# A two-layer decoder trunk on one core: late transposes, first stick-breaking scores, compressor outputs and second-branch scores stand further behind what feeds them

## The chip, the cores and the metric

The kernel runs on one core of one Trainium2 chip. The metric is the device time of one execution in microseconds. Three runs of the kernel before took 648.68, 647.72 and 650.42 us, a median of 648.68 us. One more execution was taken with the hardware profiler on; the rows below come from that one.

## The reference, cut to what matters

`x` is 256 x 1024 float32, one sequence. There are two layers, each a token mixer and an MLP, each behind an RMSNorm and added back to `x`, and a last RMSNorm.

```python
def reference(x, ...):
    for layer in range(2):
        h = rmsnorm(x, attn_norm[layer])
        x = x + (sb_diff_mixer if layer == 0 else nsa_mixer)(h, ...)
        x = x + squared_relu_mlp(rmsnorm(x, mlp_norm[layer]), mlp_w1[layer], mlp_w2[layer])
    return rmsnorm(x, final_norm)
```

Layer 0 has 8 stick-breaking heads (logits z = q k, weights exp(log sigmoid(z) + the sum of log sigmoid(-z) over later keys)) beside 4 differential heads. Layer 1 is native sparse attention: 16 heads in 4 groups with three branches, each with its own keys and values, merged by sigmoid gates: compressed blocks (blocks of 32 keys, stride 16, plus a position term, go through `gelu(flat @ w1) @ w2`), selected blocks (256 positions are 4 blocks and 16 may be taken, so all are), and a window of 512 (all positions again). Both MLPs are `square(relu(h @ w1)) @ w2` with 4096 hidden columns.

## The kernel before, in words

Everything is float32 but carried as a high and a low part: a product with a weight is three matmuls, high weight by high and by low activation and low weight by high activation. `Weights` loads each weight in halves on SP's queue, ACT casts the high part (`wh`, line 76) and DVE subtracts the low part (`wl`, line 80), some buffers ahead of use. All of TensorE's products go through `mm` (line 122), so most of its rows carry L122 and the tiles tell them apart. A scheduler works from the order in which the program issues its steps and what each waits for; it moves single instructions by a few places, so the place in the program is not all that sets the order on an engine.

Activations are kept transposed, 128 features by 256 tokens, in two token halves t=0 and t=1. After each residual add, `norm_full` or `norm_deferred` makes the scaled `xg` of one token half on DVE; `transposed` (line 408) puts four 128x128 transposes in one PSUM tile `ps_t` (line 413), ACT casts the high part and DVE subtracts the low part (lines 400 and 401). For t=0 that is done at once; for t=1 it is put on the list `late`, and `run_late` issues it among the next stage's products, so that these cover the norm of t=1.

The places that the change touches, in order of time:

- **Layer 0's mixer** (`even_mixer`): `halves(i, a, b, q, k)` projects half i of the queries and then half i of the keys of one branch, each as two tiles `ps_f` (m=0, 1) of 24 products, which ACT copies to `qsb` and `ksb` (line 647). `sb_start` issues the logits `z` of two head pairs, 16 products of 64 rows and 8 of a mask, and ACT and DVE make a softplus of them, split in high and low (`sb_e`, `sb_sp`, `sb_h`, `sb_l`, lines 717 to 722). `sb_weights` later multiplies these with a triangle of ones into the same `z`. The order is `halves(0)`, `sb_start` for pairs 0 and 1, `halves(1)`, `sb_weights`.
- **Both MLPs** (`mlp`): the first two chunks (c=0, 1) of the up projection run one token half at a time (`up_tile`, 24 products into `ps_ut`: 16 with the high weight, 8 with the low one), so that t=0 can start before t=1 is there. `run_late` issues the transposes of t=1 between (c=0, t=0) and (c=1, t=0), two groups of four. The other 14 chunks take both halves at once.
- **The entry of layer 1** (`odd_mixer`): the down projection of the first MLP (`macc`, `project_rows`) ends t by t and half by half; behind it `norm_full` and the transposes of t=0, then the value projections `ps_vs` and `ps_vw` of t=0, `run_late`, and those of t=1.
- **Layer 1's order block**: keys, queries and the two compressors (keys, then values) are projected, and softmax work of the four groups is mixed in. `run(a, b)` takes steps from two generators in turn. `scores(g, b)` issues the logits `s` of group g in branch b for both token halves, and `soft` their softmax (DVE line 1124, ACT line 1127, POOL line 1132); `cmp_scores` the compressed branch (`sc`, `pc`). `compress_blocks` projects `ps_c` (two tiles of 24 products) and transposes the positions (`ps_pos`, line 1012); `compress_hidden` gives `ps_h`; `compress_gelu` copies it out (`hc`, line 1045), adds its halves with 4 matmuls into `ps_hT` (through `fold`) and takes a gelu; `compress_keys` and `compress_values` multiply with w2 into `ps_co`. `values(i)` transposes the softmax of pair i (`pt`, line 1176; `ptc`) and issues the products with the values of pair i-1 (`o`).

```python
hk = self.compress_gelu(0, h[0], up)
run(self.compress_blocks(1, xT, up, pool, f))
run(queries(1), once(lambda: soft(scores(0, 1))))
run(self.compress_hidden(f[1], h[1]))
soft(scores(1, 0))
self.compress_keys(hk, f[0], kd)
hv = self.compress_gelu(1, h[1], up)
q2 = queries(2)
next(q2)
run(part(q2, KT))
soft(cmp_scores(0))
soft(scores(1, 1))
self.compress_values(hv, f[1], vc)
run(part(q2, KT), values(0))
```

Of the kernel before, what the change touches and what calls it, by code (L numbers as in the profile page):

```python
# [10 lines left out]
F32 = mybir.dt.float32  # L11
# [7 lines left out]
P = 128  # L19
# [80 lines left out]
class Trunk:  # L100
# [323 lines left out]
    def norm_full(self, t, n, dst):  # L424

        v = self.square_half(t, n)
        if n == 0:
            self.xg = self.tmp.tile([P, D], F32, tag="xg", name="xg")
        xg = self.xg
        self.half_gain(xg, t, n)  # L430
        if n == 0:
            return
        rs = self.rsqrt(v)
        for i in range(2):
            c = slice(i * 512, i * 512 + 512)
            self.nc.vector.tensor_scalar(xg[:, c], xg[:, c], rs, None, op0=ALU.mult)
        self.later(t, lambda: [self.transposed(t, i, xg, dst) for i in range(2)])

# [6 lines left out]

    def run_late(self):
        for f in self.late:
            f()
        self.late = []

# [30 lines left out]

    def tmajor(self, ps, w, x, t, kts, first, last, cs=slice(None)):

        wh, wl = w
        tq = slice(t * P, (t + 1) * P)
        terms = ((x[0], wh), (x[1], wh), (x[0], wl))
        for j, (a, b) in enumerate(terms):
            for i, kt in enumerate(kts):
                self.mm(ps, a[:, kt, tq], b[:, i, cs], first and i == j == 0, last and j == 2 and i == len(kts) - 1)

    def project_rows(self, o, w, act, r, t, n, first, last):

        c = slice(n * 512, n * 512 + 512)
        tq = slice(t * P, (t + 1) * P)
        for i in range(2):
            kt = 2 * r + i
            h, l = act(kt)
            self.mm(o, h[:, tq], w[0][:, i, c], kt == first, False)
            self.mm(o, h[:, tq], w[1][:, i, c], False, False)
# [9 lines left out]
    def finish_rows(self, acc, ws, act, first, last, scale, after):  # L509

        for t in range(2):
            for n in range(2):
                o = acc[t][n]
                for r, w in ws:
                    self.project_rows(o, w, act, r, t, n, first, last)
                self.add_residual(t, n, o, scale)
# [36 lines left out]
    def mlp(self, l, xT, after):  # L553
        nc = self.nc
        with self.tc.tile_pool(name=f"mlp{l}", bufs=4) as pool, \
# [23 lines left out]

            def up_tile(c, w, t):  # L580

                ps = self.bankB("ps_ut")
                self.tmajor(ps[:, :S], w, xT, t, range(8), True, True)
                r = pool.tile([P, S], F32, tag="r", name="r")
# [18 lines left out]
            for t in range(2):  # L603
                for c, w in ((0, w0), (1, w1)):
                    if len(rest) == 1 and t == 0:
                        self.run_late()
                    rest.append(up_tile(c, w, t))
                    if len(rest) > 1:
# [14 lines left out]
    def even_mixer(self, xT, oT, pool, out):  # L623
# [17 lines left out]

        def project_f(key, i, dst, scale):
            w = self.W.get((key, i))
            for m in range(2):
                ps = self.bankB("ps_f")
                self.fmajor(ps[:, :S], w, m, xT)
                nc.scalar.activation(dst[:, 2 * i + m, :], ps[:, :S], AF.Copy, scale=scale)

        def halves(i, a, b, q, k):
            project_f(a, i, q, 0.125)  # L650
            project_f(b, i, k, 1.0)
# [6 lines left out]
        with self.tc.tile_pool(name="ps_sb", bufs=2, space=PSUM) as banks:  # L658
            sb = self.sb_start((0, 1), qsb, ksb, pool, banks)
            halves(1, "sbq", "sbk", qsb, ksb)  # L660
            w = {pr: self.sb_weights(sb[pr], pool) for pr in (0, 1)}
# [150 lines left out]
    def odd_mixer(self, xT, oT, pool, out):  # L812
# [18 lines left out]
        for t in range(2):  # L831
            if t:
                self.run_late()
            ps = self.bankB("ps_vs")
            self.tmajor(ps[:, :S], ws, xT, t, range(8), True, True)
            nc.scalar.copy(v2[:, t, 0, :], ps[:, :S])
            ps = self.bankB("ps_vw")
            self.tmajor(ps[:, :304], w0, xT, t, range(4), True, False)
            self.tmajor(ps[:, :304], w1, xT, t, range(4, 8), False, True)
            nc.vector.tensor_copy(v2[:, t, 1, :], ps[:, :S])  # L840
# [20 lines left out]
        with self.tc.tile_pool(name="nsa", bufs=1) as up, \  # L861
# [56 lines left out]
            run(self.compress_hidden(f[0], h[0]))  # L918
            hk = self.compress_gelu(0, h[0], up)
            run(self.compress_blocks(1, xT, up, pool, f))  # L920
            run(queries(1), once(lambda: soft(scores(0, 1))))
            run(self.compress_hidden(f[1], h[1]))
            soft(scores(1, 0))
            self.compress_keys(hk, f[0], kd)
            hv = self.compress_gelu(1, h[1], up)
            q2 = queries(2)
            next(q2)
            run(part(q2, KT))
            soft(cmp_scores(0))
            soft(scores(1, 1))  # L930
            self.compress_values(hv, f[1], vc)
            run(part(q2, KT), values(0))
            q3 = queries(3)
            next(q3)


            run(values(1, lambda: cmp_scores(1)), part(q3, 4))
            run(values(2, lambda: scores(2, 0)), part(q3, 6))
            run(values(3, lambda: scores(2, 1)), part(q3, 6))
            rows = self.out_rows("odo", oT)  # L940
# [99 lines left out]

    def compress_gelu(self, kv, hp, up):

        nc = self.nc
        hc = up.tile([P, S], F32, tag="hc", name="hc", bufs=1)
        nc.scalar.copy(hc, hp[:, :S])
        pt = self.bankB("ps_hT")
# [162 lines left out]
    def run(self):  # L1209
        nc, a, tc = self.nc, self.a, self.tc  # L1210
        self.rs2 = {}
        self.x = self.const.tile([P, 2, D], F32, name="x")
        self.late = []
        self.weight_order()
# [91 lines left out]
```

## Time and profile before

| | |
|---|---|
| median of three runs | 648.68 us (647.72 to 650.42) |
| the profiled execution's own time | 653.47 us |
| its span | 651.8 us (1.67 us lie around it) |
| TensorE (PE) busy | 636.0 us, 98% of the span |
| VectorE (DVE) busy | 423.1 us, 65% |
| ScalarE (ACT) busy | 344.4 us, 53% |
| GpSimd (POOL) busy | 42.9 us, 7% |
| weights and data read from HBM | 106.39 MB |

A row of the timeline gives the start in us from the span's start, the busy time, the engine, the line, the operation with its output and inputs, the shapes, how many instructions of that kind stand in a row, and in brackets how long the engine had been idle before and what ended that. A busy time runs to the modelled end of the last instruction, and the next matmul starts before that end; so the length of a piece of work is best taken from its start to the start of what comes behind it. A granted clock of 1.00 is TensorE's full clock.

### The profile page before, as it was taken

What the parts mean: (1) busy time and instruction counts of PE and PEld (TensorE: products, weight loads), DVE (VectorE), ACT (ScalarE), POOL (GpSimd) and SP (SyncE); (2) the same over time, 40 slices, a digit from 0 to 9 for tenths busy, and PEclk for the clock granted to TensorE, in tenths of its full rate; (3) what the DMA queues carried; (4) which work ended last, traced back from release to release, by engine and by line L of the source; (5) the groups of instructions that cost most, each with busy time, mean ns of one, the idle gap of its engine ahead of it and who ended that gap; (6) DMA issues with size and microseconds to landing.
All of it is one profiled execution on the core that took longest, in us unless ns stands there. A gap on an engine that the chain in (4) does not pass through costs nothing.

```text
span 651.8 us, 10223 instructions
## 1 busy us (share of the span) xinstructions
PE 636.0 (98%) x3805; PEld 539.7 (83%) x3805; DVE 423.1 (65%) x863; ACT 344.4 (53%) x689; POOL 42.9 (7%) x137
## 2 busy tenths in 40 slices
PE   8999999999999999999999999999999999999995
PEld 4888997898888888888998888777888888888883
DVE  5763768786666666666876566766766666666634
ACT  4674656565444444453656554744564454445423
POOL 4000000000000000000203231440000000000000
PEclk9999999999999999999999979999999999999998
DMA  7774453375665556554798322205366565555501
GB/s 256 228 227 130 132 189 109 121 230 190 191 197 181 196 176 193 190 182 122 226 327 256 115 65 65 66 1 162 124 213 194 182 194 181 188 182 191 192 1 65
DMA packets 74132, 108.11 MB, mean 166 GB/s; under 512 B 5057, under 2 KB 60385, under 8 KB 74082
## 3 DMA queue, kind: packets, MB, share of 16 engines
q1 hardware_dynamic: 74080, 107.45, 51.4%
q8 instruction: 30, 0.49, 0.3%
q14 instruction: 20, 0.16, 0.1%
q10 hardware_dynamic: 2, 0.00, 0.0%
HBM read 106.39 MB, written 1.05 MB: 165 GB/s over the span
## 4 chain that ended last, share of the span: by engine, by line
PE 90%; DVE 3%; DMA 3%; ACT 3%; issue 1%; SPq 0%; ACTq 0%; DVEq 0%
PE macc L122 27%; PE ps_up L122 24%; PE ps_f L122 5%; PE acc L122 5%; PE ps_q L122 4%; PE ps_ut L122 3%; PE ps_v L122 3%; DMA w<-in_ev_w_in_dram 3%; PE o L122 2%; PE s L122 2%; PE ps_or L122 2%; PE ps_c L122 2%; PE pt L1176 2%; PE ps_k L122 2%; PE z L122 1%; DVE wl L80 1%
## 5 line engine op out<-in xcount | busy, mean ns | idle before, releaser
L80 DVE TENSOR_TENSOR wl<-w,wh 128x1024 fp32r<-128x1024 f32 (+1 forms) x190 | 227.0, 1212 | 122.2 <-ACT wh L76 121.9
L76 ACT CAST wh<-w 128x1024 fp32r<-128x1024 f32 (+1 forms) x188 | 191.4, 1043 | 91.9 <-PE macc L122 31.5
L122 PE MATMUL ps_up<-m,wh 128*128 128x512 f32 x448 | 159.2, 398 | 0.0
L122 PE MATMUL ps_up<-m,wl 128*128 128x256 f32 x448 | 125.7, 281 | 0.0
L122 PEld LDWEIGHTS ps_up<-m,wh 128*128 128x128 f32 x448 | 84.2, 188 | 20.3
L122 PE MATMUL macc<-wh,l 128*128 128x512 f32 x256 | 100.9, 394 | 0.0
L122 PE MATMUL macc<-wl,h 128*128 128x512 f32 x256 | 100.2, 391 | 0.0
L122 PE MATMUL macc<-wh,h 128*128 128x512 f32 x256 | 99.9, 390 | 0.0
L122 PEld LDWEIGHTS ps_up<-m,wl 128*128 128x128 f32 x448 | 84.6, 189 | 1.1
L577 ACT CAST h<-s 128x256 fp32r<-128x256 f32 x56 | 22.8, 407 | 78.8 <-DVE s L576 78.7
L122 PEld LDWEIGHTS macc<-wh,h 128*128 128x128 f32 x256 | 48.1, 188 | 10.8
L122 PEld LDWEIGHTS macc<-wl,h 128*128 128x128 f32 x256 | 48.1, 188 | 10.0
L122 PEld LDWEIGHTS macc<-wh,l 128*128 128x128 f32 x256 | 48.1, 188 | 10.0
L122 PE MATMUL ps_f<-x,wh 128*128 128x256 f32 x256 | 46.4, 284 | 0.0
L578 DVE TENSOR_TENSOR l<-s,h 128x256 fp32r<-128x256 f32 x56 | 23.8, 425 | 25.5 <-ACT h L577 25.5
L122 PEld LDWEIGHTS ps_f<-x,wh 128*128 128x128 f32 x256 | 39.9, 192 | 0.4 <-issue 0.3
L122 PE MATMUL ps_f<-x,wl 128*128 128x256 f32 x128 | 36.2, 283 | 0.0
L1132 POOL TENSOR_SCALAR p<-p,sums 128x128 f32<-128x128 f32 (+1 forms) x64 | 30.2, 491 | 88.0 <-DVE sums L1130 60.2
L1127 ACT ACTIVATE p<-p,nm 128x128 f32<-128x128 f32 (+1 forms) x64 | 28.3, 444 | 11.7 <-DVE nm L1124 10.1
L122 PE MATMUL acc<-wh,o 128*128 128x512 f32 x96 | 32.8, 407 | 0.0
L574 ACT COPY r<-ps_up 128x256 f32<-128x256 f32 x56 | 20.7, 370 | 22.5 <-PE ps_up L122 22.5
L122 PE MATMUL ps_q<-x,wh 128*128 128x256 f32 x128 | 26.7, 306 | 0.0
(255 smaller groups left out, 884.0 us busy)
## 6 DMA issues: line engine op xcount, KB each, us to landing
w<-in_mlp_w_dram SPq DMA_DIRECT2D x128, 512.0 KB, 3.8
w<-in_ev_w_in_dram SPq DMA_DIRECT2D x24, 512.0 KB, 4.9
w<-in_od_w_in_dram SPq DMA_DIRECT2D x18, 512.0 KB, 5.4
w<-in_ev_w_out_dram SPq DMA_DIRECT2D x8, 512.0 KB, 4.4
w<-in_od_w_out_dram SPq DMA_DIRECT2D x8, 512.0 KB, 4.5
cwk<-in_od_cmp_k_w_dram SPq DMA_DIRECT2D x8, 256.0 KB, 6.4
cwv<-in_od_cmp_v_w_dram SPq DMA_DIRECT2D x8, 256.0 KB, 4.4
w<-in_od_w_in_dram SPq DMA_DIRECT2D x4, 304.0 KB, 3.0
```

The lines of the kernel that those rows point to most:

```text
L76: return (self.nc.gpsimd.tensor_copy if on_pool else self.nc.scalar.copy)(h, w)
L80: return self.nc.vector.tensor_sub(l, w, h.bitcast(F32))
L122: return self.nc.tensor.matmul(out, lhsT, rhs, start=start, stop=stop, **kw)
L574: nc.scalar.copy(r, ps[:, S:])
L577: nc.scalar.copy(h, s)
L578: nc.vector.tensor_sub(lo, s, h.bitcast(F32))
L1127: nc.scalar.activation(o[:, h], o[:, h], AF.Exp, bias=nm[:, h : h + 1], scale=-1.0, accum_out=sums[:, h : h + 1])
L1132: nc.gpsimd.tensor_scalar(o[:, h], o[:, h], sums[:, h : h + 1], 0.0, op0=ALU.mult, op1=ALU.add)
L1176: nc.tensor.transpose(pt[:, h * P : (h + 1) * P], p[g, t, b][:, h, kt * P : (kt + 1) * P], self.ident)
```

## The change

Only order is changed: no operation is added or taken away, and the orders on SP and POOL, and with them all DMAs, stay the same.

- **A.** `halves` takes a function `between`, issued behind the first tile (m=0) of its queries. `sb_start` of pairs 0 and 1 is passed there: 24 products of the second query half come ahead of `z`.
- **B.** In both MLPs, the second group of four late transposes stands between the 16 high and the 8 low products of `ps_ut` (c=1, t=0), by way of `tmajor`'s new argument `mid`.
- **C.** At the entry of layer 1 the transposes of t=0 go on a list `mid` that `project_rows` empties: they come one step, which is one product in the order on TensorE, later in the last down projection. `run_late` is called between the two halves of `ps_vw`; on TensorE the scheduler leaves the late transposes where they were, behind `ps_vw`.
- **D.** `compress_out` makes the copy `hc`, and the rest of the keys' gelu is issued in the middle of the next `compress_blocks`.
- **E.** The gelu of the values' compressor is issued behind half of m=0 of `queries(2)`, `compress_values` behind m=1 and all but the last piece of `values(0)`, and `scores(1, 1)` last of all; `queries(3)` starts earlier by two steps, and the later loops take 5 of its steps, not 6, beside each `values`.

```diff
@@ norm_full
-        self.later(t, lambda: [self.transposed(t, i, xg, dst) for i in range(2)])
+        if t == 0:
+            self.mid.append(lambda: [self.transposed(t, i, xg, dst) for i in range(2)])
+        else:
+            self.late += [lambda i=i: self.transposed(t, i, xg, dst) for i in range(2)]
...
-    def run_late(self):
-        for f in self.late:
+    def run_late(self, n=2):
+        for f in self.late[:n]:
             f()
-        self.late = []
+        self.late = self.late[n:]
...
@@ tmajor
         for j, (a, b) in enumerate(terms):
+            if j == 2 and mid is not None:
+                mid()
...
@@ project_rows
             h, l = act(kt)
+            while i and mid:
+                mid.pop(0)()
...
@@ mlp
-                    if len(rest) == 1 and t == 0:
-                        self.run_late()
-                    rest.append(up_tile(c, w, t))
+                    late = c == 1 and t == 0
+                    if late:
+                        self.run_late(1)
+                    rest.append(up_tile(c, w, t, (lambda: self.run_late(1)) if late else None))
...
@@ project_f, halves
             for m in range(2):
+                if m and between is not None:
+                    between()
                 ps = self.bankB("ps_f")
...
-            sb = self.sb_start((0, 1), qsb, ksb, pool, banks)
-            halves(1, "sbq", "sbk", qsb, ksb)
+            sb = {}
+            halves(1, "sbq", "sbk", qsb, ksb, lambda: sb.update(self.sb_start((0, 1), qsb, ksb, pool, banks)))
...
@@ odd_mixer
         for t in range(2):
-            if t:
-                self.run_late()
...
             self.tmajor(ps[:, :304], w0, xT, t, range(4), True, False)
+            self.run_late()
             self.tmajor(ps[:, :304], w1, xT, t, range(4, 8), False, True)
...
-            hk = self.compress_gelu(0, h[0], up)
-            run(self.compress_blocks(1, xT, up, pool, f))
+            hc = self.compress_out(h[0], up)
+            hk = []
+            run(self.compress_blocks(1, xT, up, pool, f), once(lambda: hk.append(self.compress_gelu(0, hc, up))))
             run(queries(1), once(lambda: soft(scores(0, 1))))
             run(self.compress_hidden(f[1], h[1]))
+            hc = self.compress_out(h[1], up)
             soft(scores(1, 0))
-            self.compress_keys(hk, f[0], kd)
-            hv = self.compress_gelu(1, h[1], up)
-            q2 = queries(2)
+            self.compress_keys(hk[0], f[0], kd)
+            q2, q3 = queries(2), queries(3)
             next(q2)
-            run(part(q2, KT))
+            run(part(q2, KT // 2))
+            hv = self.compress_gelu(1, hc, up)
+            run(part(q2, KT // 2))
             soft(cmp_scores(0))
+            v0 = values(0)
+            run(part(q2, KT), part(v0, next(v0) - 1))
+            self.compress_values(hv, f[1], vc)
+            next(q3)
+            run(part(q3, 2))
+            run(part(v0, 1))
             soft(scores(1, 1))
-            self.compress_values(hv, f[1], vc)
-            run(part(q2, KT), values(0))
-            q3 = queries(3)
-            next(q3)
...
-            run(values(2, lambda: scores(2, 0)), part(q3, 6))
-            run(values(3, lambda: scores(2, 1)), part(q3, 6))
+            run(values(2, lambda: scores(2, 0)), part(q3, 5))
+            run(values(3, lambda: scores(2, 1)), part(q3, 5))
```

The order on TensorE at the start of the second MLP, before; `ps_ut` are the up products of chunk 0 (wh_4861) and chunk 1 (wh_4988, wl_4989), `ps_t_5037` and `ps_t_5044` the two groups of late transposes:

```order
L122 MATMUL ps_ut<-wh_4861,m_4846 128x256 x8
L122 MATMUL ps_ut<-wl_4862,m_4846 128x256 x8
L413 MATMUL ps_t_5037<-ident,xg 128x128 x4
L413 MATMUL ps_t_5044<-ident,xg 128x128 x4
L122 MATMUL ps_ut<-wh_4988,m_4846 128x256 x16
L122 MATMUL ps_ut<-wl_4989,m_4846 128x256 x8
```

And with the change, where the second group is called `ps_t_5061`:

```order
L122 MATMUL ps_ut<-wl_4862,m_4846 128x256 x8
L413 MATMUL ps_t_5037<-ident,xg 128x128 x4
L122 MATMUL ps_ut<-wh_4988,m_4846 128x256 x16
L413 MATMUL ps_t_5061<-ident,xg 128x128 x4
L122 MATMUL ps_ut<-wl_4989,m_4846 128x256 x8
```

The second group has moved behind 16 products; the first group stays.

The order on TensorE at the end of the keys' `compress_hidden`, before (`s_3888` are the t=0 logits of group 0, window branch; one more product of them stands 48 rows further on):

```order
L122 MATMUL ps_h_3731<-cwk_3542,fsk 64x256
L122 MATMUL ps_h_3731<-cwk_3544,fsk 64x256
L122 MATMUL s_3888<-kd,qs 128x128 x3
L122 MATMUL ps_hT<-fold,hc 128x64 x2
L1012 MATMUL ps_pos<-ident,pos 128x16
L122 MATMUL ps_c<-x_1497,wh_3619 128x256 x2
L122 MATMUL ps_c<-x_1497,wl_3620 128x256
```

With the change (`ps_pos` has the line 1026 there), from the last `ps_h` product; the pair of `ps_c` rows stands six times, 18 products in all, before `ps_hT`:

```order
L122 MATMUL ps_h_3731<-cwk_3544,fsk 64x256
L1026 MATMUL ps_pos<-ident,pos 128x16
L122 MATMUL ps_c<-x_1497,wh_3619 128x256 x2
L122 MATMUL ps_c<-x_1497,wl_3620 128x256
...
L122 MATMUL ps_hT<-fold,hc 128x64 x2
```

`ps_hT` now stands behind 18 products of `ps_c`, and the logits `s_3888` in one piece further on.

The order on TensorE at the values' compressor and the second branch of group 1, before (`sc_4081` compressed logits of group 0; `s_4104` and `s_4112` the second-branch logits of group 1, t=0 and t=1; `ps_q` with wh_3857 the queries of group 2; each `ps_co` row is one of eight small products):

```order
L122 MATMUL sc_4081<-kd,qs 128x16 x8
L122 MATMUL s_4104<-kd,qs 128x128 x4
L122 MATMUL ps_co<-w2v,hT_4038 128x64
L122 MATMUL ps_q<-x_1497,wh_3857 128x256 x2
L122 MATMUL ps_q<-x_1497,wl_3858 128x256
L122 MATMUL ps_co<-w2v,hT_4041 128x64
L122 MATMUL s_4112<-kd,qs 128x256 x4
L122 MATMUL ps_co<-w2v,hT_4038 128x64
```

With the change (`pt_4106` is the first transpose of `values(0)`, `s_4177` and `s_4185` the same logits of group 1, wh_4029 the queries of group 3):

```order
L122 MATMUL sc_4081<-kd,qs 128x16 x8
L122 MATMUL ps_q<-x_1497,wh_3857 128x256 x2
L122 MATMUL ps_q<-x_1497,wl_3858 128x256
L1193 MATMUL pt_4106<-ident,p 128x128 x4
...
L122 MATMUL ps_co<-w2v,hT_4062 128x64
L122 MATMUL ps_co<-w2v,hT_4065 128x64
L122 MATMUL ps_q<-x_1497,wh_4029 128x256 x2
L122 MATMUL ps_q<-x_1497,wl_4030 128x256
...
L1202 MATMUL ptc_4171<-ident,pc_3182 128x128
L122 MATMUL s_4177<-kd,qs 128x128 x4
L122 MATMUL s_4185<-kd,qs 128x256 x4
```

Between `sc_4081` and the first `ps_co` there now stand the 24 products of the second tile of `ps_q` (group 2) and two groups of transposes; the eight `ps_co` are in one piece, and both logits of group 1 come behind 6 products of group 3's queries.

## Rows read from the trace of the kernel before

**Rows 1.** The page: busy time per engine; TensorE's clock in 40 slices.

```profile
PE 636.0 (98%) x3805; PEld 539.7 (83%) x3805; DVE 423.1 (65%) x863; ACT 344.4 (53%) x689; POOL 42.9 (7%) x137
PEclk9999999999999999999999979999999999999998
```

**Rows 2.** TensorE's waits by releaser: us in total, times, longest us.

```profile
PE ps_t L413 <- DVE v L381: 1.3, 2, 1.1
...
PE z L122 <- ACT ksb L647: 1.1, 1, 1.1
...
PE ps_co L122 <- PE s L122: 0.9, 1, 0.9
PE ps_hT L122 <- ACT hc L1045: 0.8, 1, 0.8
```

**Rows 3.** Windows from 380 us: length; busy us by engine; PEclk, DMA share, GB/s.

```profile
380.00:382.00 2.00, 1.12 (x15) 0.96 (x13) 1.97 (x8) 0.00 (x0) 1.73 (x4) 1.00 0.00 0
382.00:392.00 10.00, 10.00 (x48) 9.06 (x47) 4.55 (x28) 5.26 (x20) 2.06 (x6) 0.50 0.01 2
392.00:394.00 2.00, 2.00 (x17) 1.75 (x18) 0.42 (x1) 0.87 (x1) 1.23 (x3) 0.92 0.00 0
```

**Rows 4.** Timeline around the first stick-breaking scores, TensorE and VectorE.

```profile
37.21 0.92 PE L122 MATMUL z<-qsb,ksb 64*128 64x256 f32 x8
39.27 0.92 PE L122 MATMUL z<-qsb,ksb 64*128 64x256 f32 x8 [1.14 <-ACT ksb L647]
40.55 0.48 PE L122 MATMUL ps_f<-x,wh 128*128 128x256 f32 x2
...
46.97 1.82 DVE L722 TENSOR_TENSOR sb_l<-sb_sp,sb_h 128x768 fp32r<-128x768 f32 x2
...
52.15 0.34 PE L122 MATMUL z<-sb_h,negU 128*128 128x384 f32 x1
```

**Rows 5.** Chain that ended last, layer 0: start, us, what.

```profile
60.51 2.06 PE z L122 x24
...
72.01 11.55 PE ps_f L122 x96
```

**Rows 6.** Timeline at the start of the second MLP, TensorE and VectorE.

```profile
464.91 0.60 PE L413 MATMUL ps_t<-ident,xg 128*128 128x128 f32 x4
466.63 0.63 PE L413 MATMUL ps_t<-ident,xg 128*128 128x128 f32 x4 [1.12 <-DVE v L381]
467.01 2.16 PE L122 MATMUL ps_ut<-wh,m 128*128 128x256 f32 x16
...
468.05 1.28 DVE L401 TENSOR_TENSOR m<-ps_t,m 128x512 fp32r<-128x512 f32 x2
```

**Rows 7.** TensorE's timeline at the entry of layer 1, transposes of t=0.

```profile
308.63 1.06 PE L413 MATMUL ps_t<-ident,xg 128*128 128x128 f32 x8 [0.23 <-DVE xg L436]
309.45 0.48 PE L122 MATMUL macc<-wh,l 128*128 128x512 f32 x1
```

**Rows 8.** Window at the entry of layer 1, columns as in rows 3.

```profile
310.40:318.20 7.80, 7.80 (x56) 7.42 (x56) 7.76 (x18) 4.96 (x11) 3.69 (x41) 1.00 0.57 143
```

**Rows 9.** Timeline at the keys' compressor, ScalarE and TensorE.

```profile
355.56 0.37 ACT L1045 COPY hc<-ps_h 128x256 f32<-128x256 f32 x1
...
355.99 0.66 PE L122 MATMUL ps_hT<-fold,hc 128*128 128x64 f32 x4 [0.80 <-ACT hc L1045]
```

**Rows 10.** Chain that ended last, layer 1: start, us, what.

```profile
345.64 1.51 PE s L122 x16
...
364.91 1.28 PE s L122 x7
```

**Rows 11.** Timeline at the values' compressor and the second branch, VectorE and TensorE.

```profile
380.95 0.72 DVE L1069 TENSOR_TENSOR hT<-ps_hT,gel 128x240 f32<-128x240 f32 x2
...
381.46 0.41 PE L122 MATMUL ps_co<-w2v,hT 128*128 128x64 f32 x2 [0.88 <-PE s L122]
...
407.79 0.66 PE L1176 MATMUL pt<-ident,p 128*128 128x128 f32 x4 [0.20 <-DVE pT L1179]
```

More of the change, by code (lines that the diff above doesn't have):

```diff
@@ L480, in fmajor_wide, with tmajor @@
             self.mm(ps[:, :S], wl[:, kt, c], x[0][:, kt, :], False, kt == KT - 1, skip_group_check=True)
-    def tmajor(self, ps, w, x, t, kts, first, last, cs=slice(None)):
+    def tmajor(self, ps, w, x, t, kts, first, last, mid=None):
         wh, wl = w
@@ L487, in tmajor, with project_rows @@
         for j, (a, b) in enumerate(terms):
+            if j == 2 and mid is not None:
+                mid()
             for i, kt in enumerate(kts):
-                self.mm(ps, a[:, kt, tq], b[:, i, cs], first and i == j == 0, last and j == 2 and i == len(kts) - 1)
-    def project_rows(self, o, w, act, r, t, n, first, last):
+                self.mm(ps, a[:, kt, tq], b[:, i], first and i == j == 0, last and j == 2 and i == len(kts) - 1)
+    def project_rows(self, o, w, act, r, t, n, first, last, mid=()):
         c = slice(n * 512, n * 512 + 512)
@@ L514, in finish_rows @@
                 for r, w in ws:
-                    self.project_rows(o, w, act, r, t, n, first, last)
+                    self.project_rows(o, w, act, r, t, n, first, last, self.mid if t == n == 1 else ())
                 self.add_residual(t, n, o, scale)
@@ L578, in up, with up_tile @@
                     nc.vector.tensor_sub(lo, s, h.bitcast(F32))
-            def up_tile(c, w, t):
+            def up_tile(c, w, t, mid=None):
                 ps = self.bankB("ps_ut")
-                self.tmajor(ps[:, :S], w, xT, t, range(8), True, True)
+                self.tmajor(ps[:, :S], w, xT, t, range(8), True, True, mid)
                 r = pool.tile([P, S], F32, tag="r", name="r")
@@ L640, in project_v, with project_f @@
             nc.scalar.copy(dst[:, 1, :], pss[1])
-        def project_f(key, i, dst, scale):
+        def project_f(key, i, dst, scale, between=None):
             w = self.W.get((key, i))
             for m in range(2):
+                if m and between is not None:
+                    between()
                 ps = self.bankB("ps_f")
@@ L647, in project_f, with halves @@
                 nc.scalar.activation(dst[:, 2 * i + m, :], ps[:, :S], AF.Copy, scale=scale)
-        def halves(i, a, b, q, k):
-            project_f(a, i, q, 0.125)
+        def halves(i, a, b, q, k, between=None):
+            project_f(a, i, q, 0.125, between)
             project_f(b, i, k, 1.0)
@@ L1039, in compress_hidden, with compress_out, compress_gelu @@
             yield 1
-    def compress_gelu(self, kv, hp, up):
+    def compress_out(self, hp, up):
+        hc = up.tile([P, S], F32, tag="hc", name="hc", bufs=1)
+        self.nc.scalar.copy(hc, hp[:, :S])
+        return hc
+    def compress_gelu(self, kv, hc, up):
         nc = self.nc
-        hc = up.tile([P, S], F32, tag="hc", name="hc", bufs=1)
-        nc.scalar.copy(hc, hp[:, :S])
         pt = self.bankB("ps_hT")
@@ L1212, in run @@
         self.x = self.const.tile([P, 2, D], F32, name="x")
-        self.late = []
+        self.late, self.mid = [], []
         self.weight_order()
```

## The prediction

> **What bounds the kernel now.** Read first the page's busy times: TensorE works for 636.0 of 651.8 us, no other engine for more than 65% [rows 1]. So the time is TensorE's products plus the gaps between them, and an order can win only gaps, slow stretches of TensorE, and starts and ends of short pieces. Second, TensorE's waits by releaser [rows 2]: four gaps of about a microsecond or a little less lie at places that the change touches, 1.1 of `ps_t` behind the norm (of 1.3 in two waits, so the other is 0.2), 1.1 of `z` behind ScalarE's copy of `ksb`, 0.9 of `ps_co`, 0.8 of `ps_hT` behind the copy `hc`. Together 4.1 us. Third, the clock: one slice of forty shows 7 instead of 9 [rows 1], and the windows say where: the granted clock is 1.00 in 380 to 382, 0.50 in all of 382 to 392, and 0.92 in 392 to 394 [rows 3]. At half clock this is the 1.2 GHz level, at full the 2.4 GHz one. 0.08 of the last two microseconds, at half a clock short, is 0.3 us, so the stretch is about 10.3 us long, and work that fills all of it (10.00 busy of 10.00) would take half of that at full clock: it costs 10.3 / 2 = 5.1 us. It begins right behind the wait of `ps_co`.
>
> That matters for what is compared. The profiled execution took 653.47 us, 4.8 above the median of 648.68. Without the half-clock stretch it would have been 653.47 - 5.1 = 648.4, which is the median within 0.3. I take it, therefore, that the timed runs mostly don't hold this stretch. Their own spread, 647.72 to 650.42, is 2.7, too little for a stretch of 5.1 in some and none in others. The sum is made against the profiled execution's own time; its part without the clock carries over to the median.
>
> **A, first scores.** From the first `z` row to the first projection behind the mask products is 40.55 - 37.21 = 3.34 us [rows 4]. The same 24 products in one piece, with nothing to wait for, take 2.06 [rows 5]. The difference, 1.28, is the wait of 1.14 and a second start. The change puts 24 projection products ahead: 96 of them take 11.55, so 24 take 2.9 [rows 5]. `z` then starts at about 37.2 + 2.9 = 40.1, and its wait for `ksb` ended at 39.27: covered with 0.8 to spare. What becomes late next: the softplus starts where `z` ends, at about 42.1 instead of 40.5, 1.6 later; `sb_l` ends at 46.97 + 1.82 = 48.8 now and at 50.4 then, and its readers at 52.15 move up to 50.9, since 1.28 is gone [rows 4]. That holds by 0.5 us. Saved: **1.28**. Bounds: 0.8, if DVE takes `sb_l` 0.5 later than that margin allows; 1.3.
>
> **B, late transposes.** In the second MLP two groups of four take 467.01 - 464.91 = 2.10 us with the wait of 1.12 in them [rows 6]; eight transposes in one piece take 309.45 - 308.63 = 0.82 [rows 7]. Difference 1.28, less some 0.1 for a second start among the `ps_ut` products: **1.2**. The cover: the 16 `ps_ut` products take 2.16 with the tail of the last one, about 2 us [rows 6], so the second group comes at 465.3 + 2.0 = 467.3, and it was free to start at 466.63. Next in line: its high part and then its low part must be there before t=1's products reach them. VectorE now does the low parts of both groups from 468.05 to 469.33 [rows 6]; with the group 0.7 later the second ends at some 470. The 8 low products and chunk 0's first eight high ones (16 products, 2 us) lie between, to about 469.8, and the low parts of the second group come four products later, so this is just met. I keep 0.9 as the lower bound. In the first MLP the wait is only 0.2 [rows 2], and I count **0.2** there.
>
> **C, entry of layer 1.** The wait of 0.23 ahead of the t=0 transposes [rows 7] goes. But the next stretch has VectorE busy for 7.76 of 7.80 us [rows 8], and what it makes there, the low part of t=0 and the norm of t=1, ends the stretch: it starts when the last residual is added, and the transposes of t=1 wait for it at the same time as before. What is won before is waited for behind. **0**, bounds -0.2 to 0.2. The move of `run_late` into `ps_vw` changes nothing on TensorE, since the order there stays.
>
> **D, keys' compressor.** `hc` ends at 355.93 and `ps_hT` starts at 355.99 after 0.80 of idling [rows 9]. Eighteen products (18 x 11.55 / 96 = 2.2 us) now come first, which start at about 355.2 and end at 357.4: cover of 1.4. The logits, now in pieces of which the later one takes 1.28 for 7 rows, were in the group before one piece of 1.51 for 16 [rows 10]; I add 0.1 for that. `ps_hT` ends some 1 us later than now; the gelu and the `ps_co` of the keys have all of `queries(1)` before them. **0.9**, bounds 0.6 to 1.0.
>
> **E, values' compressor and second branch.** The wait of 0.88 goes: `hT` (its first half is ready at about 381.4 [rows 11]) is followed by 24 products of group 2's queries, 2.9 us, before the first `ps_co`. Against that, these 24 products were cover for the transposes of `values(0)`, and 6 more of group 3 are used up early. The stretch that follows is a chain of logits, softmax on VectorE, ScalarE and POOL, and transposes, in which `pt` waits already (0.20 [rows 11]); I give back 0.5 for about 0.7 us of cover (6 products) that is missing there. **0.4**, bounds -0.8 (a wait of a `pt` as long as the longest here, 1.1 to 1.2 [rows 2]) and 0.9.
>
> **The clock.** The fall stands right behind the wait of `ps_co`, in a window where TensorE was busy 1.12 of 2.00 us [rows 3]; the waits of 1.14 at 39, 0.80 at 355 and 1.12 at 466 are as long and no fall follows them, as the single 7 among the 9s shows [rows 1]. So the wait alone doesn't do it; it came on top of products of 16 columns. I expect the changed order, in which neither the wait nor that mixture is left, to keep the full clock: **5.1** in the profiled execution, nothing in timed runs that never had the stretch. The Trainium skill ("TensorE: Matmul & The Clock Gate", the section on HAM oscillation) tells of a clock that drops in waits for transfers which are much longer than this one; by it a wait of 0.88 us would not be the cause, the stretch could stay, and the profiled execution would come out at 649.5 rather than 644.4. No run so far shows which.
>
> **Sum.** 1.28 + 1.2 + 0.2 + 0 + 0.9 + 0.4 = 4.0 us. Profiled execution: 653.47 - 5.1 - 4.0 = 644.4. Timed: 648.68 - 4.0 = 644.7; I say **644.6**. The lower bounds add up to 1.3 and the upper ones to 4.8, but they will not all fall together.
>
> **Rivals.**
>
> 1. *The timed runs hold the half-clock stretch too, and lose it.* For it: the profile is all we have of the clock, and a profiled execution may be slower by several us for other reasons. Against it: 653.47 - 5.1 meets the median. Time: 648.68 - 4.0 - 5.1 = 639.6. Chance 0.2.
> 2. *Layer 1 gives its part back.* The softmax chain on VectorE, ScalarE and POOL from 380 to 410 bounds that stretch, not TensorE's waits one by one; D and E then win nothing, and the next `pt` or `o` waits longer by what was won. For it: VectorE is busy 1.97 of 2.00 in 380 to 382 [rows 3] and `pt` waits already at 407.79 [rows 11]. Against: VectorE is busy only 4.55 of 10 in 382 to 392, though at half a clock for TensorE. Time: 648.68 - 1.28 - 1.2 - 0.2 = 646.0. Chance 0.18.
> 3. *Slower: the clock falls in the changed kernel where the timed runs held it.* Place: the eight `ps_co` of 64 columns are now in one piece, and the logits of 64 rows come behind a transpose that waits for `pc`; if that stretch is as thin as 380 to 382 (TensorE busy for 1.12 of 2.00 [rows 3]), the same fall follows. Price: 5.1, and where D and E are lost as well: 648.68 - 2.7 + 5.1 = 651.1. It decides from the point where the new waits there sum to the 0.88 that went. Chance 0.07; with a second or a longer fall beside it (a further 2 us) it would pass 651.9.
> 4. *The scheduler undoes it.* That the order on TensorE moved is seen for A, B, D and E, and not for the second half of C; so this rival is left only for C, and holds nothing in the sum.
>
> The forecast itself, with its terms within their bounds, has 0.55: its own range is 643.4 to 646.0.
>
> **How the numbers follow.** 0.5% is 3.2 us, about what a measurement of this kernel can tell from no change; faster by that means below 645.4. From the forecast case some four fifths, 0.44, and all of rival 1, 0.20, are faster: 0.64. Rival 2 and the rest of the forecast case, and rival 3 where it adds up to less than 651.9, are the same: 0.32. Slower: 0.04, the worst of rival 3 and of E's lower bound with it. The range takes in rival 1 (639.6, less 0.5) and rival 2 (646.0, and 1.4 more for a `pt` wait as in E's lower bound): 639.1 to 647.4. It leaves out rival 3 and the tails, some 0.15.
>
> **What would show it.** In the profile after: no wait of `z` for `ksb`, and the softplus's readers without a wait of `sb_l`; of `ps_t` behind the norm no wait over 0.3; none of `ps_hT` and `ps_co`; the clock at 9 in all slices but the ends; TensorE's waits at `pt`, `ptc` or `o` in layer 1 at most 0.7 in total. Wrong would be: a half-clock stretch still there or elsewhere; a profiled time over 648 without one; new waits of half a microsecond or more at `z<-sb_h`, at t=1's `ps_ut`, or at `pt` and `o` of groups 0 and 1. A median near 640 with a clean profile before of the same would be rival 1.

## The result

The changed kernel takes 642.40 us (median of 6 runs, 640.75 to 643.01), against 650.82 for the kernel before in the 6 runs beside it and ahead of it (647.72 to 654.03). The ratio on record is 0.9885, with a 95% interval of 0.9855 to 0.9915: faster by 1.15%, or about 7.5 us (5.5 to 9.4 by the interval) where 4.0 was forecast. The ratio isn't the quotient of these two medians, which lie 8.4 us apart. The time lies in the stated range of 639.1 to 647.4, but under the forecast's own range of 643.4 to 646.0. Run again later, beside other kernels, it gave 642.09 and a ratio of 0.9877 (0.9844 to 0.991).

The page after, the parts that answer to [rows 1]; the span is 640.4 us and the profiled execution's own time 642.12:

```profile
PE 628.7 (98%) x3805; PEld 534.3 (83%) x3805; DVE 422.7 (66%) x863; ACT 344.9 (54%) x689; POOL 44.2 (7%) x137
PEclk9999999999999999999999999999999999999998
```

The work is the same (3805 products), TensorE's busy time is 7.3 us less, and no slice shows 7 any more. TensorE's four longest waits after, in the columns of [rows 2]:

```profile
PE ps_warm L122 <- DVE zero L130: 1.3, 1, 1.3
PE ps_v L122 <- ACT x L210: 0.5, 1, 0.5
PE ptc L1202 <- DVE pT L1196: 0.4, 1, 0.4
PE pt L1193 <- DVE pT L1196: 0.4, 1, 0.4
```

All four waits of [rows 2] are gone; two of 0.4 at `ptc` and `pt` are new, 0.8 together where the prediction allowed 0.7. The windows that answer to [rows 3]:

```profile
378.00:382.00 4.00, 4.00 (x37) 4.00 (x36) 3.42 (x9) 2.06 (x4) 0.00 (x0) 1.00 0.00 0
382.00:392.00 10.00, 10.00 (x96) 7.95 (x96) 8.34 (x36) 7.50 (x24) 3.43 (x8) 1.00 0.35 107
```

Full clock, and 96 products in 10 us where 48 stood. TensorE's timeline after at the four places, which answers to [rows 4], [rows 6], [rows 9] and [rows 11]:

```profile
39.12 1.58 PE L122 MATMUL z<-qsb,ksb 64*128 64x256 f32 x16
...
41.05 0.48 PE L122 MATMUL ps_f<-x,wh 128*128 128x256 f32 x2
...
354.27 0.55 PE L122 MATMUL ps_hT<-fold,hc 128*128 128x64 f32 x4
...
379.75 1.89 PE L122 MATMUL ps_co<-w2v,hT 128*128 128x64 f32 x16
...
397.70 0.66 PE L1193 MATMUL pt<-ident,p 128*128 128x128 f32 x4 [0.40 <-DVE pT L1196]
...
454.85 0.60 PE L413 MATMUL ps_t<-ident,xg 128*128 128x128 f32 x4
455.20 2.16 PE L122 MATMUL ps_ut<-wh,m 128*128 128x256 f32 x16
457.20 0.60 PE L413 MATMUL ps_t<-ident,xg 128*128 128x128 f32 x4
```

None of the moved pieces carries a wait in brackets; the only one in these rows is a transpose of the softmax.

Where the time went is read best from stages. For ten profiles the table gives the time from the start of one product to the start of another, each taken from TensorE's timeline. "Start" is the first `ps_f`; A from there to the first `z<-sb_h`; B1 to the first `ps_up`; C to t=1's first `ps_vs`; D from the first `ps_h` of the keys to the first of the values; E on to the first `ps_or`; B2 on to the second MLP's first `ps_up`.

| kernel | start | A | B1 | C | D | E | B2 |
|---|---|---|---|---|---|---|---|
| before | 25.47 | 26.68 | 91.03 | 176.20 | 19.03 | 50.06 | 56.37 |
| the change | 24.63 | 25.14 | 90.61 | 176.20 | 17.76 | 44.02 | 55.10 |
| A alone (single run) | 26.06 | 25.14 | 90.99 | 176.17 | 19.03 | 45.33 | 56.41 |
| B alone | 24.32 | 27.22 | 90.63 | 176.19 | 19.02 | 45.34 | 55.10 |
| D alone (single run) | 25.84 | 27.19 | 91.00 | 176.17 | 17.76 | 44.97 | 56.40 |
| D alone (timed) | 25.17 | 26.62 | 91.02 | 176.20 | 17.77 | 45.00 | 56.37 |
| E alone | 22.53 | 29.38 | 91.02 | 176.30 | 19.02 | 44.02 | 56.40 |
| change without C, E | 26.28 | 25.14 | 90.62 | 176.16 | 17.77 | 44.98 | 55.09 |
| change without A | 23.77 | 27.36 | 91.02 | 176.17 | 17.76 | 44.02 | 55.10 |
| queries later | 24.52 | 25.14 | 90.66 | 176.19 | 17.78 | 43.18 | 55.08 |

Of the 11.4 us between the two profiled spans, 0.84 is the start, which the change doesn't touch; A is 1.54, B 0.42 and 1.27, C 0, D 1.27, and E 6.04, of which the half-clock stretch is 50.06 - 45.33 = 4.7 and order 45.33 - 44.02 = 1.31.

### The profile page after: what moved, and what is told of

The parts are those of the page before. It is cut to its first block, busy times and chain, and to the rows that moved or that the text cites. A ratio compares the mean times of both kernels' runs of the same rounds, so it can differ in the third digit from the quotient of the medians.

```text
span 640.4 us, 10224 instructions
## 1 busy us (share of the span) xinstructions
PE 628.7 (98%) x3805; PEld 534.3 (83%) x3805; DVE 422.7 (66%) x863; ACT 344.9 (54%) x689; POOL 44.2 (7%) x137
## 4 chain that ended last, share of the span: by engine, by line
PE 95%; DVE 1%; ACT 1%; DMA 1%; issue 0%; SPq 0%; DVEq 0%; ACTq 0%
PE macc L122 28%; PE ps_up L122 25%; PE ps_f L122 7%; PE acc L122 5%; PE ps_v L122 4%; PE ps_ut L122 4%; PE ps_q L122 3%; PE o L122 2%; PE ps_or L122 2%; PE ps_c L122 2%; PE ps_k L122 2%; PE s L122 1%; PE pt L1193 1%; PE z L122 1%; PE ps_h L122 1%; PE ps_vw L122 1%
## 5 line engine op out<-in xcount | busy, mean ns | idle before, releaser
L1149 POOL TENSOR_SCALAR p<-p,sums 128x128 f32<-128x128 f32 (+1 forms) x64 | 31.5, 512 | 79.7 <-DVE sums L1147 66.2
```

The lines of the kernel that those rows point to most:

```text
L1149: nc.gpsimd.tensor_scalar(o[:, h], o[:, h], sums[:, h : h + 1], 0.0, op0=ALU.mult, op1=ALU.add)
```

## The experiments

The gain was nearly twice the forecast, so the question was what the rest is. Theory 1: timed executions of before hold half-clock stretches too, and the change is rid of them. Theory 2: they hardly do, and the order is worth more than the sum said. Each run of a kernel also has its mean granted clock. In the runs of these kernels it falls into three groups, 0.996 or more, 0.992 to 0.995, and 0.991 or less:

| kernel | runs | 0.996 or more | 0.992 to 0.995 | 0.991 or less |
|---|---|---|---|---|
| before, three sets | 57 | 28 (mean 647.81 us) | 15 (650.30) | 14 (652.42) |
| the change, both sets | 12 | 12 (642.13) | 0 | 0 |
| A alone | 12 | 5 | 0 | 7 |
| D alone | 12 | 8 | 4 | 0 |
| E alone | 12 | 7 | 5 | 0 |
| half of E | 12 | 5 | 6 | 1 |
| change without C, E | 6 | 6 | 0 | 0 |
| change without A | 6 | 5 | 1 | 0 |

So the profiled execution of before, with a clock of 0.989, wasn't the exception: 29 of 57 runs hold a lower clock, and cost 2.5 or 4.6 us more. The mean of all 57 is 649.60, so this is 1.8 us of the time before. The groups are cut by hand, and the lowest holds more than one size: the nine runs of before at 0.988 to 0.990 cost 5.6 us, the five at 0.991 cost 2.9.

**E alone.** The edit is that of the change from `hc = self.compress_out(h[1], up)` to the 5 in `part(q3, 5)`, with the keys' gelu left at its place:

```diff
-            hk = self.compress_gelu(0, h[0], up)
+            hk = self.compress_gelu(0, self.compress_out(h[0], up), up)
```

> The kernel before with part E alone (values' compressor, second-branch scores, earlier queries). The two traces put E's place at 6.04 us, of which 5.1 would be the half-clock stretch and 0.94 order. Theory 1: the stretch belongs to the old order around ps_co, and timed executions of the kernel before hold it too, some wholly, some in part; then E alone gives 0.9 and some 2 to 3 us, a ratio of 0.994 to 0.996, its times spread less than those of before, and its profile shows full clock in all slices. Theory 2: only the profiled execution held the stretch, and the timed gain is the order of all parts; then E alone gives 0.9 us, a ratio near 0.9985, with times that spread as those of before.

Measured: 646.98 us, ratio 0.9963 (0.9941 to 0.9986), E's stage 44.02. E's stage came out as in the change. The ratio lies between the two theories, and its interval takes in both 0.996 and 0.9985, so the time alone doesn't decide. The clocks say more: none of the 12 runs is in the lowest group, where 14 of 57 of before are. Full clock in all slices, which theory 1 expected, did not come. The fall sat elsewhere, behind a wait of `z` that was twice as long here as in [rows 4]. ScalarE's and TensorE's timeline there:

```profile
36.13 1.04 ACT L76 CAST wh<-w 128x1024 fp32r<-128x1024 f32 x1 [1.88 <-DMA w<-in_ev_w_in_dram]
37.08 0.38 ACT L647 ACTIVATE ksb<-ps_f 128x256 f32<-128x256 f32 x1
...
37.51 1.27 PE L122 MATMUL z<-qsb,ksb 64*128 64x256 f32 x8 [2.29 <-ACT ksb L647]
```

and the windows, columns as in rows 3:

```profile
36.00:38.00 2.00, 0.49 (x4) 0.47 (x6) 0.79 (x1) 1.65 (x3) 0.00 (x0) 0.99 0.91 297
38.00:40.00 2.00, 2.00 (x16) 1.70 (x15) 1.66 (x2) 1.37 (x2) 0.00 (x0) 0.50 0.90 293
40.00:42.00 2.00, 2.00 (x14) 2.00 (x13) 0.00 (x0) 2.00 (x4) 0.00 (x0) 0.66 0.89 267
```

TensorE waits for ScalarE's copy of `ksb`, but the copy waits behind a cast of a later weight, and the cast for that weight's transfer, while the DMA engines are 91% busy. So the size of this wait is set here by the weight's arrival, not by ScalarE. In five of the other six profiles without A the cast ahead of that copy waits for a transfer too (0.7 to 1.5 us); in the single run of D alone it waits 1.0 for VectorE.

**The change without C and E.** A, B and D stay as they are; the order from `hv` on is that of before, with the copy `hc` in a function of its own, which D needs:

```diff
-            hv = self.compress_gelu(1, h[1], up)
+            hv = self.compress_gelu(1, self.compress_out(h[1], up), up)
             q2 = queries(2)
             next(q2)
             run(part(q2, KT))
             soft(cmp_scores(0))
             soft(scores(1, 1))
             self.compress_values(hv, f[1], vc)
             run(part(q2, KT), values(0))
```

> The change without part E and without C: A, B and D. By the two traces A is worth 1.55, B 0.41 and 1.27, D 1.28, in all 4.5 us, a ratio of 0.993 by both theories. Theory 1: its times spread as those of before (6 us from lowest to highest), and its profile may show a half-clock stretch of about 10 us behind the wait of ps_co, at about 375 to 388 us. Theory 2: narrow times, full clock.

Measured: 643.88 us, ratio 0.9913 (0.9883 to 0.9942): by the ratio 5.6 us less than before, by the medians 4.6; the stages A, B and D explain 4.5. All six clocks are 0.996 or more, and the times spread over 3.0 us, not the 6 of theory 1. So E doesn't seem to be needed to be rid of the lower clocks, against theory 1; with six runs that is likely rather than certain.

**A alone and D alone, a single run each.** The edits are parts A and D of the diff, nothing else.

> The kernel before with part A alone. By the traces the path from the first ps_f to the first z from sb_h is 1.55 us shorter, and all behind it moves up by as much; the wait of z for ksb is gone and none of sb_l takes its place. Theory 1: the profile is likely to show the half-clock stretch near 381 to 391 us, as before. Theory 2: full clock there.

> The kernel before with part D alone. By the traces the stretch from ps_h of the keys to ps_h of the values is 1.28 us shorter: the wait of 0.80 gone, the rest from the logits in one piece. If the softmax chain gave it back, less than 0.5. Theory 1: half-clock stretch behind the wait of ps_co near 380 us; theory 2: full clock.

Measured: 647.76 and 647.93 us, both at full clock throughout. A's stage 25.14 and no wait for `sb_l`; D's stage 17.76, 1.27 less. Nothing gives D back; what came unasked is that E's stage is 0.36 shorter with D, since the wait of `ps_co` falls from 0.87 to 0.51. One run says nothing of the clock: this execution of A held no fall, and seven of the next twelve did.

**The change without A; A alone, timed.**

> The change without part A. Theory 1: half-clock stretches come from two places, the wait of z for ksb (about 40 us in; ScalarE's copy stands behind a cast that waits for a weight transfer, 1.1 to 2.3 us in the profiles so far) and the wait of ps_co (about 380 us); without A only the first is left. Then some four runs in ten show a mean clock of 0.993 to 0.995, none shows 0.991 or less, and the times lie 1.5 to 4 us above those of the change with more spread; a ratio to before of 0.993 to 0.996. Theory 2: the lower clocks have no place in the program but come and go with the execution; then this kernel shows the mix of before, or none as the change did, and is 1.5 us slower than the change.

> The kernel before with part A alone, timed. Theory 1: no run with a clock of 0.993 to 0.995, since the wait of z is gone; some one in four with 0.988 to 0.991, from the wait of ps_co of 0.87, each some 5 us above the others. The others lie 1.5 to 2.5 us below the runs of before that have a clock of 0.997 or more. Ratio 0.995 to 0.998. Theory 2: the same mix of clocks as before, 1.5 us lower.

Measured without A: 643.51, ratio 0.9891 (0.9857 to 0.9925), 1.1 to 1.4 us above the change's two medians, with one clock of 0.995 and none lower; the wait of `z` in its profile is 1.9. So a long wait of `z` doesn't always bring a fall. Theory 1 had expected a lower clock in some four runs of ten and a ratio of 0.993 to 0.996. (B1's 0.4 is missing in this profile, where `ps_utt` comes 0.40 later behind the products ahead of it, with 0.24 shown as a wait.) A alone: 648.46, ratio 0.9978 (0.9952 to 1.0005), which can't be told from none: seven of its runs hold a clock of 0.991 or less, a larger share than of before. Six of these seven have 0.991, and the seven take 2.5 us more than the other five, not the 5 that was expected. The five at full clock lie 0.7 us under those of before, not 1.5 to 2.5; they are few, and in the profiles the start alone varies between 22.5 and 26.3. The middle group is empty in it, as theory 1 said of a kernel in which `z` doesn't wait. Its profile, with a clock of 0.991, holds a fall at the old place:

```profile
378.00:380.00 2.00, 1.12 (x15) 0.96 (x16) 1.94 (x7) 0.00 (x0) 1.84 (x4) 1.00 0.00 0
380.00:390.00 10.00, 10.00 (x59) 9.18 (x59) 5.14 (x29) 5.46 (x21) 2.52 (x7) 0.66 0.01 2
```

The same 1.12 busy microseconds of 2.00 stand ahead of it as in [rows 3]. But the fall is shorter: a mean clock of 0.66 over 10 us is 6.8 us at half clock, where [rows 3] has about 10.3. In E's stage it costs 48.56 - 45.33 = 3.2 us.

**Half of E.** The values' gelu and the compressor's output move; the logits and group 3's queries stay.

```diff
+            hc = self.compress_out(h[1], up)
             soft(scores(1, 0))
             self.compress_keys(hk, f[0], kd)
-            hv = self.compress_gelu(1, h[1], up)
             q2 = queries(2)
             next(q2)
-            run(part(q2, KT))
+            run(part(q2, KT // 2))
+            hv = self.compress_gelu(1, hc, up)
+            run(part(q2, KT // 2))
             soft(cmp_scores(0))
             soft(scores(1, 1))
+            run(part(q2, KT), values(0))
             self.compress_values(hv, f[1], vc)
-            run(part(q2, KT), values(0))
```

> The kernel before with the first half of E: the values' gelu and ps_co moved back, scores(1,1) left at their old place, no earlier queries. The wait of ps_co is gone. Theory 1: no clock of 0.991 or less; 0.993 to 0.995 in some four of ten as in the kernel with E alone, from the wait of z. Ratio 0.996 to 0.999. If instead the products of 16 columns and 64 rows ahead of ps_co bring the clock down, and not its wait, some runs of 0.988 to 0.991 remain. Path from the values' ps_h to the first ps_or: 44.0 us if the moved compressor brings all of E's gain, 44.9 if the scores' move brings it.

Measured: 649.27, ratio 0.9991 (0.9962 to 1.0021): nothing won. The wait of `ps_co` is gone, yet one run has 0.990 and six lie in the middle group. The profile is one of these, 0.995: `z` waited 1.8 in it without a fall, and the fall comes at 389. So neither group belongs to one wait, as theory 1 had it:

```profile
384.00:388.00 4.00, 3.65 (x37) 3.19 (x36) 3.43 (x17) 3.78 (x12) 2.22 (x6) 1.00 0.02 4
388.00:390.00 2.00, 2.00 (x15) 2.00 (x15) 1.74 (x3) 0.37 (x1) 2.00 (x3) 0.74 0.00 0
390.00:392.00 2.00, 2.00 (x11) 1.04 (x11) 0.00 (x0) 1.90 (x3) 0.12 (x1) 0.50 0.71 211
392.00:394.00 2.00, 2.00 (x16) 1.47 (x13) 1.90 (x4) 0.58 (x2) 0.00 (x0) 0.91 0.15 51
```

What stands ahead of it, in TensorE's timeline:

```profile
385.53 0.33 PE L1190 MATMUL ptc<-ident,pc 128*128 128x128 f32 x1 [0.35 <-DVE pc L1170]
...
386.03 1.07 PE L122 MATMUL sc<-kd,qs 64*128 64x16 f32 x16
386.94 0.47 PE L122 MATMUL s<-kd,qs 64*128 64x128 f32 x2
387.34 2.24 PE L122 MATMUL ps_co<-w2v,hT 128*128 128x64 f32 x16
```

A wait of 0.35, then products of 16 columns, of 64 rows and of 64 columns in a row, with no wait among them; so the wait of `ps_co` isn't what the fall needs. The clocks of these windows add up to 3.4 us at half clock.

E's stage is 46.66 here. Half of 3.4 us is the fall's cost by an estimate, so without it the stage would be about 45.0, against 45.33 in the profiles of A alone and B alone: the moved compressor by itself brings little of E's gain. In place of the wait of `ps_co` stand three smaller ones, 0.36 at `s`, 0.35 at `ptc` and 0.45 at `pt` (0.20 in before).

**Part B alone; D alone, timed.**

> The kernel before with part B alone. By the traces 0.41 us less on the path from the first z from sb_h to the first ps_up, 1.27 less from the first ps_or to the second MLP's first ps_up, and nothing else moved: waits of z, ps_hT and ps_co as before. A new wait at t=1's ps_ut would make it less.

> The kernel before with part D alone, timed. Its profile shows the wait of ps_co at 0.5 instead of 0.9, with the same short products around it. If the half-clock stretch near 380 us needs both, the short products and that wait, then no run, or one, has a clock of 0.991 or less, where 9 of 40 runs of before and 7 of 12 with A alone had it; clocks of 0.993 to 0.995 from the wait of z stay in some. If the short products alone bring it, some 4 of 12 runs show 0.991 or less.

Measured: B alone 646.46 in a single run, with 0.40 and 1.27 less in its stages and the waits of `ps_hT` and `ps_co` as before; `z` waited 1.7. D alone 647.19, ratio 0.9958 (0.9931 to 0.9984), with no clock of 0.991 or less in 12 runs (nor in the 6 of the change without C and E, which has D too), and 4 of 0.995. The short products are the same as in A alone; the wait among them is 0.5, not 0.87.

**The change again, and group 3's queries kept for later.** In the change, `pt` and `ptc` wait in `values(2)` and `values(3)`; the edit gives these loops a step more.

```diff
-            run(values(1, lambda: cmp_scores(1)), part(q3, 4))
-            run(values(2, lambda: scores(2, 0)), part(q3, 5))
-            run(values(3, lambda: scores(2, 1)), part(q3, 5))
+            run(values(1, lambda: cmp_scores(1)), part(q3, 2))
+            run(values(2, lambda: scores(2, 0)), part(q3, 6))
+            run(values(3, lambda: scores(2, 1)), part(q3, 6))
```

> The change, with values(1) taking 2 steps of queries(3) instead of 4 and values(2) and values(3) taking 6 instead of 5. The change's two waits of 0.4 at pt and ptc lie in values(2) and values(3). If cover is what is missing there, they go, and the path from the values' ps_h to the first ps_or falls from 44.0 to about 43.3. If VectorE's and ScalarE's softmax chain sets them, they come back in values(1), and the path stays at 44.0 or grows to 44.5.

> The change again, beside queries_timed on the same chip. If its gain over before is order (A 1.5, B 0.41 and 1.27, D 1.27, E 0.95: 5.4 us) plus half-clock stretches that it no longer has (1.3 to 1.8 us in the mean of before), it lies 6.5 to 7.5 us under before, a ratio of 0.988 to 0.990, and no run has a clock under 0.996. If the first comparison owed something to its chip, the ratio is 0.991 or more.

> The change with group 3's queries kept for values(2) and values(3), timed. By its profile it is 0.84 us shorter on the path from the values' ps_h to the first ps_or. It should lie 0.5 to 1.2 us under the change, with clocks of 0.996 or more. If its better time in one look was the start alone (which varies by some 3 us between executions), no difference.

Measured: a single run gave 641.21 and E's stage 43.18, 0.84 less; both waits are gone. Timed beside the change on one chip it took 640.59 (640.47 to 642.17), the change 642.09 (641.08 to 643.24); ratios to before 0.9859 (0.9823 to 0.9894) and 0.9877. The 1.5 us between the two medians is somewhat more than the 0.5 to 1.2 expected. Its waits, but for one of 0.2 at `odf` in layer 0:

```profile
PE ps_warm L122 <- DVE zero L130: 1.3, 1, 1.3
PE ps_v L122 <- ACT x L210: 0.7, 1, 0.7
PE ps_t L191 <- DVE xg L184: 0.4, 1, 0.4
PE ps_vs L122 <- ACT x L400: 0.2, 1, 0.2
```

The change came out again close to where its order and the lost half-clock stretches put it (0.988 to 0.990), with no clock under 0.996, and "queries later" is the fastest version measured here.

## Why the prediction was right, and where it fell short

Every part of the change did its work where the prediction said, and each was worth what was forecast or more: 5.8 us of order where the sum has 4.0. That the time lies in the stated range is owed to the range and not to the sum: it had been stretched to take in rival 1.

- **A** was forecast at 1.28 and is 1.54 between the two profiles. The cover was right, and nothing waits for `sb_l`. The 24 products of `z` take 41.05 - 39.12 = 1.93 us after, not the 2.06 of [rows 5]; the other 0.13 is in the projections around them. The step also took 1.14 [rows 2, 4] for the wait, and that is one sample: in the seven profiles without A that stage takes 26.6 to 29.4, with A 25.1 in each of seven. Without A the first `z<-sb_h` starts at 51.1 to 53.0 while the first `ps_f` starts at 22.5 to 25.8, since the wait of `z` takes up part of an early start; with A it follows the start.
- **B**: 0.2 and 1.2 forecast, 0.42 and 1.27 measured. In the first MLP I counted the wait and left out the second start that I had reckoned with in the second.
- **C**: 0 forecast, 0 measured, for the reason given. The wait of 0.23 ahead of the t=0 transposes is gone, but those of t=1 start 0.6 us behind the start of VectorE's `xg` as before, and the wait of 0.24 for `x` behind them is the same. Before, and then after:

```profile
317.44 0.88 DVE L436 TENSOR_SCALAR xg<-xg,rs 128x512 f32<-128x512 f32 x2
318.08 1.06 PE L413 MATMUL ps_t<-ident,xg 128*128 128x128 f32 x8
319.38 0.73 PE L122 MATMUL ps_vs<-wh,x 128*128 128x256 f32 x4 [0.24 <-ACT x L400]
...
314.64 0.88 DVE L436 TENSOR_SCALAR xg<-xg,rs 128x512 f32<-128x512 f32 x2
315.27 1.06 PE L413 MATMUL ps_t<-ident,xg 128*128 128x128 f32 x8
316.58 0.61 PE L122 MATMUL ps_vs<-wh,x 128*128 128x256 f32 x3 [0.24 <-ACT x L400]
```

- **D**: 0.9 forecast, 1.27 in its own stage and 0.36 in E's. Beyond the wait of 0.80, the logits in one piece and the new place of `ps_hT` were worth 0.47 together, where I gave them 0.1.
- **E**: 0.4 forecast. Alone it is 45.33 - 44.02 = 1.31; behind D 0.96. The giving back that I priced at 0.5 is there, 0.4 and 0.4 at `pt` and `ptc`, and "queries later" shows that it was cover: two steps of queries at the right place win 0.84. The gross gain was therefore some 2.1, of which the wait of 0.88 is less than half. The rest I hadn't seen; that short pieces now stand in fewer and longer runs would explain it, but wasn't tried by itself.
- **The clock** is the step that was wrong. That the changed order keeps the full clock came true in all of 12 runs, and the stretch in the profile of before was worth 4.7 where 5.1 was reckoned; wrong was what the timed runs hold. "I take it, therefore, that the timed runs mostly don't hold this stretch" rested on one profile that met the median, and on a spread of 2.7 in three runs. In 57 runs 29 hold a lower clock, 1.8 us in the mean, because the stretch comes in several lengths and in about half the runs, so that three of them can look alike. That is rival 1, at a third of its price; rivals 2 and 3 didn't come. (The lower bounds of the sum add up to 1.5 with the first MLP's 0.2, not to 1.3.)

The account closes. Among runs with a clock of 0.996 or more the difference is 647.81 - 642.13 = 5.7; the stages give 1.54 + 0.42 + 1.27 + 1.27 + 1.31 = 5.8, with A's wait as the one profile of before had it. With the 1.8 of the lower clocks it is 7.5, which is what the ratio says.

What brings the clock down is only half settled. Measured: with A alone the middle group is empty in 12 runs, where it holds 15 of 57 of before; with D the lowest group is empty in 18 (12 alone, 6 beside A and B), where it holds 14 of 57. Shown too: neither the wait of `z` (1.9 and 1.8 without a fall, 2.3 with one) nor that of `ps_co` (gone, and a fall all the same) decides by itself. Four of the fourteen profiles hold a fall. Ahead of it stand a wait of 0.88 behind products of 16 columns and of 64 rows (before and A alone), a wait of 2.29 (E alone), and a wait of 0.35 with such short products behind it (half of E). In the same kernel a fall comes in one execution and not in the next; what tips it stays open. The Trainium skill ("TensorE: Matmul & The Clock Gate", the section on HAM oscillation) ties the drop to much longer waits, for transfers. The traces don't agree that it takes those: ahead of the fall of about 10.3 us in the profile of before, the longest wait is 0.88.

## What to carry to other kernels

Where an engine is 98% busy, its few waits are still worth reading one by one: here four of them fell to longer cover and paid more than their own length (1.14 gave 1.54, 1.12 gave 1.27, 0.80 gave 1.27, 0.88 gave 1.31, with other moves beside it), while the wait that C took away paid nothing, since VectorE set what came behind it. Part of the surplus is the counting: a wait is counted from the modelled end of the product ahead, and 0.24 shown at `ps_utt` was 0.40 from start to start. Whether a short piece that starts anew costs more by itself wasn't tried. Ask of a wait what sets it behind the engine that it names: if a transfer does, its length in one profile is one sample, and the cover should fit the longest of several. Read the granted clock of every run before a profile's slow stretch is called an exception; it told apart groups of times that a median had mixed.

## What the runs showed of the hardware

In a stream that keeps TensorE busy 98% of the time, the granted clock fell to 0.50 (the 1.2 GHz level) for about 10.3 us at 382 us into the kernel, with no idle stretch of over 0.9 us anywhere near. The other three falls that were traced lasted 6.8, 3.4 and 3.4 us. Runs with a lower mean clock take 2.5 or 4.6 us more in the mean of their group and are 29 of 57 of the same program; a different order of the same products has none in 12.
